# A two-layer decoder trunk: five plain gate/up pairs a layer in place of six, and two plain query/key groups in head one in place of three

## The chip, the cores and the metric

The kernel runs on one core of one Trainium2 chip. The time is the device time of one execution in microseconds (us). A core has TensorE for matmuls (PE in the profile, its weight loads PEld), VectorE (DVE), ScalarE (ACT), GpSimd (POOL) and SyncE (SP), which work side by side, each through its own queue of instructions in order, and 16 DMA engines that move data between HBM and the on-chip memory. Matmuls write to PSUM, of which the kernel keeps eight tiles of 128x512.

## The reference

512 tokens of width 1024 pass through an attention layer and a pooling layer, each followed by a SwiGLU feed-forward net of hidden width 2816. All of it is in float32.

```python
def reference(x, ...):
    for i in range(2):
        if i == 0:
            x = x + dilated_attention_mixer(rmsnorm(x, attn_norm), w_qkv, w_attn_out)
        else:
            x = x + pooling_mixer(rmsnorm(x, pool_norm), w_pool_in, w_pool_group, pool_scale)
        x = x + swiglu_ffn(rmsnorm(x, ffn_norm[i]), w_ffn_gate_up[i], w_ffn_down[i])
    return rmsnorm(x, final_norm)

def swiglu_ffn(h, w_gate_up, w_down):
    gu = h @ w_gate_up
    gate, up = gu[..., :D_FF], gu[..., D_FF:]
    return (jax.nn.silu(gate) * up) @ w_down
```

The attention mixer has eight head slots. Each slot has three groups (dilation 1, 4 and 16) with their own queries, keys and values; the three results of a slot are merged with weights from their softmax denominators, and one output projection follows.

## The kernel before

Activations lie with features on the 128 partitions and the 512 tokens along the columns, in eight tiles of 128 features. To keep nearly float32 accuracy with operands in fp32r, every operand is split into a high and a low half (`split`, L77 on ACT for the high half, L78 on DVE for the low one), and a product is three matmuls: high by high, high by low, low by high.

**Two ways to make a pair of output tiles.** A pair is two tiles of 128 features by 512 tokens: a gate tile and its up tile, or the queries and keys of a group.

- *Plain* (`product`, lines L254 to L257): eight feature tiles times three matmuls of 512 columns for each output tile, 48 matmuls for the pair. Its weights come in two loads of 512 KB (`Plain`, L113) and need two splits of 128x1024.
- *Strassen* (`seven`, `mult`, lines L368 to L370; in the values of attention L481 to L483): the pair, the features and the tokens are each cut in halves, and seven products of half size replace eight. Each is four feature tiles times three matmuls of 256 columns: 84 matmuls. The weights come in three loads by SP (L134 to L136) and one by POOL that adds onto one of them in flight (L137, an accumulating DMA). They need three splits of 128x1024 and one of 128x512, and two additions on DVE between (L150, L151). DVE then joins the seven products (L409, L417, L422, L423).

Strassen also needs sums and differences of the normalized input. `prepare(k)` makes them for feature tiles k and k+4, for k from 0 to 3: two normalizations (L431), three additions (L435 to L437) and their splits (`h` and `t`, `tx` in attention; `tb`, `tt`, `tn` in the feed-forward nets). The scratch of `prepare(k)` is two buffers of the same ring of four that the weights land in (`raw`).

**What sets the order.** `Plain` and `Pair` put their loads and splits in queues when the program is laid out. `pump`, which is called after products, issues the next loads if their buffers are free, and the next split if one of the five buffers for split weights (`w`) is. A scheduler then orders each engine's instructions. In the trace an instruction that waits holds up all behind it on its engine.

**Attention.** Head 0 is plain. In head one the first `NSOLO` groups are plain, the others Strassen; its values and all later heads are Strassen. Between the products other work of the previous and the present head is put in by `between(h, g)`. In head one, after the first group comes `merge(0)`: TensorE exchanges the softmax sums (L618), DVE works out the weights (L620 to L630) and scales head 0's probabilities with them (L632 for `s0`, L635 on ACT for `s12`). At the third group come `turn0(0)`, seven transposes of `s0` on TensorE (L644), `turn12(0)` (L654, L657) and `scores0(1)` (L562 to L573). Behind a plain group these are laid out when both of its products are done. In `seven` they are put behind its first, third and fifth product. `scores12(1)` (L588) stands behind the first product of head one's values.

**Feed-forward net.** Of 22 gate/up pairs a layer the first `NPLAIN` are plain and the others Strassen. Two output tiles and the start of a third are already made before the normalization factor `row` is there (`lead`). `plain_pair` scales gate and up by `row` (L899, L905), and `activation` applies SiLU, multiplies (L868) and splits the result (`a`). `prepare(0)` to `prepare(3)` are laid out behind plain pairs 1 to 4. After 11 pairs the down projection of that half follows.

Of the kernel before, what the change touches and what calls it, by code (L numbers as in the profile page):

```python
# [32 lines left out]
NF = 4  # L33
H2 = S // 2
K2 = KC // 2
NPLAIN = 6
WARM = 6
NSOLO = 3
DOWN = (6, 5)
BUFS = {"w": 5, "half": 2, "raw": 4, "rawhalf": 2}  # L40
COLS = {"w": D, "half": D // 2, "raw": D, "rawhalf": D // 2}
# [7 lines left out]
def trunk(ctx: ExitStack, tc: tile.TileContext, xT, norms, w_first, w_qk, w_qkp, w_v0, w_v0p, w_v12, w_out, w_pair, w_down, w_pin, w_pgrp,  # L49
# [26 lines left out]
    def split(hi, lo, v):  # L76
        nc.scalar.activation(hi, v, AF.Copy)  # L77
        nc.vector.tensor_tensor(lo, v, hi.bitcast(F32), op=OP.subtract)  # L78
# [96 lines left out]
    def pairs(*srcs):  # L175

        these = [Pair(src) for src in srcs]
        for parts in zip(*(p.steps() for p in these)):
            steps.extend(parts)
        units.append(these)  # L180

    def plain_gu(layer, j):
        src = w_pair[layer, j]
        units.extend([Plain(src[:, S:3 * S]), Plain(src[:, 3 * S:], src[:, :S])])

    def plain(*srcs):
        units.extend([Plain(src) for src in srcs])

    for h in range(HEADS):
        if h == 0:  # L190
            plain(*[w_qk[u] for u in range(len(QK) - NF)])
        for g in range(3):
            if h == 1 and g < NSOLO:
                plain(*[w_qk[len(QK) - NF + 2 * g + c] for c in range(2)])
            elif h:
                pairs(w_qkp[3 * h - 3 - NSOLO + g])
        if h == 0:
# [7 lines left out]
    def ffn_plan(layer):  # L205
        for hf in range(2):
            for j in range(hf * HALF, (hf + 1) * HALF):
                if j < NPLAIN:
                    plain_gu(layer, j)
# [55 lines left out]
    def slot(name, dtype=F32R):  # L265
        i = free.popleft()
        t = pools[i].tile([P, 2, S], dtype, tag=f"slot{i}", name=name, bufs=1)
        return i, t
# [3 lines left out]
    def give(key):  # L272
        free.append(held.pop(key))
# [6 lines left out]
    def product(layer):  # L280
        return Product(KC, stream(layer)).add(range(KC)).p
# [23 lines left out]
    def note(layer, k):  # L305

        if layer < 4:
            held[layer, k], t = slot("h")
            scaled(layer, k, t[:, 0], t[:, 1])
        square(layer, k)  # L310
# [115 lines left out]
    def normed(layer, k, row):  # L426

        h, t = Held("raw"), Held("raw")
        for i in range(2):
            c = k + i * K2  # L430
            nc.vector.scalar_tensor_tensor(h.t[:, i * S:(i + 1) * S], X[c], nrm[:, layer, c:c + 1], row,  # L431
                                           op0=OP.mult, op1=OP.mult)
        hq = h.t.rearrange("p (a b c) -> p a b c", a=2, b=2)
        tq = t.t.rearrange("p (a b c) -> p a b c", a=2, b=2)
        nc.vector.tensor_sub(tq[:, :, 0], hq[:, :, 1], hq[:, 0])  # L435
        nc.vector.tensor_sub(t.t[:, H2:S], t.t[:, :H2], h.t[:, 3 * H2:])
        nc.vector.tensor_add(t.t[:, 3 * H2:], t.t[:, H2:S], h.t[:, S:3 * H2])  # L437
        return h, t
# [10 lines left out]
    with tc.tile_pool(name="opool", bufs=1) as opool:  # L449
        early = opool.tile([P, HEADS, S], F32R, tag="o", name="early")  # L450
        with tc.tile_pool(name="apool", bufs=1) as apool:
# [340 lines left out]
            for h in range(1, HEADS):  # L792
                for g in range(3):
                    if h == 1 and g < NSOLO:
                        for c in range(2):
# [58 lines left out]
    with tc.tile_pool(name="fpool", bufs=2) as fpool:  # L854
# [5 lines left out]
        def ftile(name, n=S):  # L860
            return fpool.tile([P, PAD + S], F32, tag="f", name=name, bufs=6)[:, :n]
# [3 lines left out]
        def activation(gt, up):  # L865

            nc.scalar.activation(gt, gt, AF.Silu)
            nc.vector.tensor_mul(up, up, gt)  # L868
            j = len(act)
            held["a", j], t = slot("a")  # L870
            act.append((t[:, 0], t[:, 1]))
            split(*act[-1], up)

        def unfold(m, p):

            if m == 0:
                held["x", 0], t = slot("xs", F32)
                new = t[:, 0]
            else:
                new = x_tile(m - 1)  # L880
            for b in range(NT):
                nc.vector.tensor_add(new[:, b * P:(b + 1) * P], *(
                    t.rearrange("p (r j i b) -> p b i j r", r=NT, j=NT, b=NT)[:, b] for t in (X[m], p)))
            X[m] = new

        def ffn(layer, nxt, lead, row):

            op = nxt - 1

            def gu():  # L890
                return lead.pop(0).p if lead else product(op)

            def hidden(j):
                return act[j]

            def plain_pair(last):
                pg = gu()
                gt = ftile("gt")
                nc.vector.tensor_mul(gt, pg, row)  # L899
                pu = gu()  # L900
                if last:
                    for k in range(KC):
                        give((op, k))
                up = ftile("up")
                nc.vector.tensor_mul(up, pu, row)  # L905
                activation(gt, up)

            T = {}

            def prepare(k):  # L910


                h, t = normed(op, k, row)
                hq, b22 = h.t.rearrange("p (a b c) -> p a b c", a=2, b=2), h.t[:, 3 * H2:]
                held["t", k, 0], b = slot("tb")
                split(b[:, 0].rearrange("p (a c) -> p a c", a=2), b[:, 1].rearrange("p (a c) -> p a c", a=2), hq[:, :, 0])
                T["11", k], T["21", k] = (tuple(b[:, e, i * H2:(i + 1) * H2] for e in range(2)) for i in range(2))
                for i, names in enumerate((("1", "2"), ("3", "4"))):
                    held["t", k, 1 + i], b = slot("tt")
                    split(b[:, 0], b[:, 1], t.t[:, i * S:(i + 1) * S])  # L920
                    for a, name in enumerate(names):
                        T[name, k] = tuple(b[:, e, a * H2:(a + 1) * H2] for e in range(2))
                if k % 2 == 0:
                    held["t", k, 3], T["n"] = slot("tn")
                n = tuple(T["n"][:, e, k % 2 * H2:(k % 2 + 1) * H2] for e in range(2))
                split(*n, b22)
                T["22", k] = n
                h.done()
                t.done()

            def strassen_pair():
                gt, up = ftile("gt"), ftile("up")
                seven(T, gt, up, ftile)
                activation(gt, up)

            for hf in range(2):
                act.clear()
                for j in range(hf * HALF, (hf + 1) * HALF):
                    if j < NPLAIN:
                        plain_pair(j == NPLAIN - 1)  # L940
                        if 0 < j <= K2:
                            prepare(j - 1)
                    else:
                        strassen_pair()
                early = [Product(HALF, hidden).add(range(HALF - 1)) for i in range(2)]
                if hf:
                    for key in [key for key in held if key[0] == "t"]:
                        give(key)
                for m in range(KC - 2 if nxt == 4 and hf else KC):
                    if early:  # L950
                        f = early.pop(0).add([HALF - 1])
                    else:
                        f = Product(HALF, hidden).add(range(HALF))
                    if hf and layer == 0:
                        unfold(m, f.p)
                    else:
                        nc.vector.tensor_add(X[m], X[m], f.p)
                    if hf:
                        note(nxt, m)
                if not (hf and nxt == 4):  # L960
                    for j in range(HALF):
                        give(("a", j))
            return hidden

        lead = begin(2, 1, range(KC - 1))
        row = finish(lead, 1, [KC - 1])
        ffn(0, 2, lead, row)
        moved = x_tile(KC - 1)
        nc.scalar.copy(moved, X[0])
# [73 lines left out]
        for f in lead:  # L1043
            f.add(range(2, 4))
        row = finish(lead, 3, range(2))
        hidden = ffn(1, 4, lead, row)


# [122 lines left out]
```

## Time and profile before

| | |
|---|---|
| median of 3 runs | 1260.09 us (1259.58 to 1260.82) |
| profiled execution | 1261.29 us, span of its instructions 1259.5 us |
| granted TensorE clock, mean | 0.996 |
| PE, PEld, DVE, ACT, POOL busy | 1247.1, 1149.4, 927.3, 563.6, 123.0 us |

Where the stages lie in the span (us from its start), by the matmuls' lines:

| stage | from | to |
|---|---|---|
| head 0 | 0 | 57.45 |
| head one, plain groups 1 to 3 | 57.45 | 90.49 |
| head one, transposes and scores between | 90.49 | 93.13 |
| head one's values, heads 2 to 7 | 93.13 | 438.26 |
| output projection | 438.26 | 489.80 |
| layer 0, plain gate/up pairs | 489.80 | 557.36 |
| layer 0, five Strassen pairs | 557.36 | 607.83 |
| layer 0, down; 11 Strassen pairs; down | 607.83 | 838.44 |
| pooling | 838.44 | 911.98 |
| layer 1, rest of the plain pairs | 911.98 | 964.47 |
| layer 1, five Strassen pairs | 964.47 | 1015.54 |
| layer 1, down; 11 Strassen pairs; down; end | 1015.54 | 1259.5 |

A row of a timeline reads: start, duration, engine, line, operation, output<-inputs, shapes, count, and in brackets how long the engine sat idle before it and what ended that. A matmul's duration is longer than the time it takes in a row of matmuls, since they overlap. So TensorE's pace is read from one start to the next. The same holds on DVE, with smaller overlaps. Rows of a window give busy time and count for each engine, then the granted TensorE clock, the mean busy share of the DMA engines and GB/s.

### The profile page before, as it was taken

How to read it: one execution, taken by the hardware profiler on the slowest of the kernel's cores; microseconds unless marked ns; L12 is line 12 of the kernel's file. 1: busy time of each engine (PE TensorE's matmuls, PEld its weight loads, DVE VectorE, ACT ScalarE, POOL GpSimd, SP SyncE). 2: the span in 40 equal slices, each digit the busy share in tenths (PEclk: the TensorE clock that was granted, in tenths of full speed). 3: DMA queues.
4: the chain of work that ended last, by engine and by line, in shares of the span. 5: the costliest groups of instructions: out<-in, count | busy, mean ns of one | idle time of the engine just before them, and what ended most of it. 6: DMA issues, size and time to landing. Idle time of an engine off the chain costs nothing.

```text
span 1259.5 us, 20807 instructions
## 1 busy us (share of the span) xinstructions
PE 1247.1 (99%) x8262; PEld 1149.4 (91%) x8262; DVE 927.3 (74%) x1415; ACT 563.6 (45%) x871; POOL 123.0 (10%) x121
## 2 busy tenths in 40 slices
PE   9999999999999999999999999999999999999997
PEld 7889999999999988889889999888788988999987
DVE  6987888878879854788537887559878854788643
ACT  6445554544546543445324554343444532455331
POOL 1111111211111100000001110001300000110000
PEclk9999999999999999999999999999999999999998
DMA  8336556656656532246456764333124645676322
GB/s 284 114 85 172 131 158 165 146 144 164 162 143 151 181 122 83 85 112 173 126 142 170 181 180 120 103 134 118 57 72 110 176 125 141 168 187 163 92 69 68
DMA packets 67330, 172.45 MB, mean 137 GB/s; under 512 B 6928, under 2 KB 9120, under 8 KB 67232
## 3 DMA queue, kind: packets, MB, share of 16 engines
q1 hardware_dynamic: 48816, 135.97, 33.6%
q0 software_dynamic: 17264, 34.09, 15.9%
q8 instruction: 65, 1.06, 0.3%
q10 hardware_dynamic: 1152, 1.05, 0.3%
q14 instruction: 33, 0.27, 0.1%
HBM read 168.99 MB, written 2.10 MB: 136 GB/s over the span
## 4 chain that ended last, share of the span: by engine, by line
PE 80%; issue 11%; DVE 6%; DMA 1%; POOL 1%; ACT 1%; SPq 0%; POOLq 0%; DVEq 0%; ACTq 0%
PE ps L369 13%; PE ps L368 13%; PE ps L370 13%; PE ps L254 9%; PE ps L255 9%; PE ps L257 9%; PE ps L481 2%; PE ps L482 2%; PE ps L483 2%; DVE wlo L78 1%; PE ps L678 1%; PE ps L588 1%; DMA raw<-w_pair 1%; DVE n L302 1%; POOL rcol L323 1%
## 5 line engine op out<-in xcount | busy, mean ns | idle before, releaser
L77 ACT ACTIVATE whi<-raw 128x1024 fp32r<-128x1024 f32 (+2 forms) x297 | 296.2, 1002 | 429.3 <-PE ps L255 193.1
L78 DVE TENSOR_TENSOR wlo<-raw,whi 128x1024 fp32r<-128x1024 f32 (+2 forms) x297 | 341.1, 1152 | 137.2 <-ACT whi L77 135.2
L254 PE MATMUL ps<-a,whi 128*128 128x512 f32 (+1 forms) x374 | 141.0, 377 | 0.0
L255 PE MATMUL ps<-a,whi 128*128 128x512 f32 (+1 forms) x374 | 140.9, 377 | 0.0
L257 PE MATMUL ps<-a,wlo 128*128 128x512 f32 (+1 forms) x374 | 140.8, 377 | 0.0
L368 PE MATMUL ps<-tt,whi 128*128 128x256 f32 x384 | 108.7, 283 | 0.0
L369 PE MATMUL ps<-tt,whi 128*128 128x256 f32 x384 | 108.7, 283 | 0.0
L370 PE MATMUL ps<-tt,wlo 128*128 128x256 f32 x384 | 108.7, 283 | 0.0
L137 POOL DMA_DIRECT2D raw<-w_pair x32 | 38.7, 1210 | 445.9 <-DVE wlo L78 182.3
L257 PEld LDWEIGHTS ps<-a,wlo 128*128 128x128 f32 x374 | 70.4, 188 | 13.0
L254 PEld LDWEIGHTS ps<-a,whi 128*128 128x128 f32 x374 | 70.4, 188 | 12.7
L255 PEld LDWEIGHTS ps<-a,whi 128*128 128x128 f32 x374 | 70.4, 188 | 12.7
L368 PEld LDWEIGHTS ps<-tt,whi 128*128 128x128 f32 x384 | 73.7, 192 | 0.0
L369 PEld LDWEIGHTS ps<-tt,whi 128*128 128x128 f32 x384 | 73.7, 192 | 0.0
L370 PEld LDWEIGHTS ps<-tt,wlo 128*128 128x128 f32 x384 | 73.7, 192 | 0.0
L369 PE MATMUL ps<-tb,whi 128*128 128x256 f32 x256 | 72.6, 284 | 0.4 <-DVE tb L78 0.4
L368 PE MATMUL ps<-h,whi 128*128 128x256 f32 x252 | 72.5, 288 | 0.0
L370 PE MATMUL ps<-tb,wlo 128*128 128x256 f32 x256 | 72.4, 283 | 0.0
L368 PE MATMUL ps<-tb,whi 128*128 128x256 f32 x256 | 72.4, 283 | 0.0
L370 PE MATMUL ps<-h,wlo 128*128 128x256 f32 x252 | 71.3, 283 | 0.0
L369 PE MATMUL ps<-h,whi 128*128 128x256 f32 x252 | 71.3, 283 | 0.0
L254 PE MATMUL ps<-h,whi 128*128 128x512 f32 x160 | 62.7, 392 | 0.0
(281 smaller groups left out, 3412.8 us busy)
## 6 DMA issues: line engine op xcount, KB each, us to landing
raw<-w_pair SPq DMA_DIRECT2D x76, 512.0 KB, 4.4
raw<-w_qkp SPq DMA_DIRECT2D x36, 512.0 KB, 4.1
raw<-w_pair POOLq DMA_DIRECT2D x32, 512.0 KB, 7.3
raw<-w_down SPq DMA_DIRECT2D x32, 384.0 KB, 3.1
raw<-w_down SPq DMA_DIRECT2D x32, 320.0 KB, 2.8
raw<-w_v SPq DMA_DIRECT2D x18, 512.0 KB, 4.4
raw<-w_qkp POOLq DMA_DIRECT2D x18, 512.0 KB, 7.2
rawhalf<-w_pair SPq DMA_DIRECT2D x32, 256.0 KB, 3.3
```

Source lines behind the costliest of these rows:

```text
L77: nc.scalar.activation(hi, v, AF.Copy)
L78: nc.vector.tensor_tensor(lo, v, hi.bitcast(F32), op=OP.subtract)
L137: nc.gpsimd.dma_start(self.b.t.rearrange("p (a c) -> p a c", a=2), self.src[:, None, 3 * S:].to_broadcast([P, 2, S]), accum_op=OP.add)
L254: nc.tensor.matmul(self.p[:, cols], w[0][:, s], mh[:, cols], start=self.done == 0, stop=False)
L255: nc.tensor.matmul(self.p[:, cols], w[0][:, s], ml[:, cols], start=False, stop=False)
L257: nc.tensor.matmul(self.p[:, cols], w[1][:, s], mh[:, cols], start=False, stop=self.done == self.n)
L368: nc.tensor.matmul(dst, w.t[0][:, c], th, start=k == 0, stop=False)
L369: nc.tensor.matmul(dst, w.t[0][:, c], tl, start=False, stop=False)
L370: nc.tensor.matmul(dst, w.t[1][:, c], th, start=False, stop=k == K2 - 1)
L481: nc.tensor.matmul(o, mh, wh, start=k == 0, stop=False)
L482: nc.tensor.matmul(o, mh, wl, start=False, stop=False)
L483: nc.tensor.matmul(o, ml, wh, start=False, stop=k == K2 - 1)
```

## The change

`NPLAIN` goes from 6 to 5: gate/up pair 5 of each layer is made by Strassen. `prepare(0)` to `prepare(3)` are laid out behind plain pairs 0 to 3. `NSOLO` goes from 3 to 2: the third group of head one (dilation 16) is made by Strassen.

```diff
-NPLAIN = 6
+NPLAIN = 5
 WARM = 6
-NSOLO = 3
+NSOLO = 2
...
                     if j < NPLAIN:
                         plain_pair(j == NPLAIN - 1)
-                        if 0 < j <= K2:
-                            prepare(j - 1)
+                        if j < K2:
+                            prepare(j)
                     else:
                         strassen_pair()
```

The three places at which instructions move, engine by engine:

TensorE, end of head one's third group, before (`s_509` is head 0's `s0`, `L254` to `L257` the plain product):

```order
L254 MATMUL ps<-early,whi 128x512
L255 MATMUL ps<-early,whi 128x512
L257 MATMUL ps<-early,wlo 128x512
L644 MATMUL ps<-ident,s_509 128x128 x7
L654 MATMUL ps<-ident,s_598 128x128 x4
L562 MATMUL ps<-qk_699,qk_668 128x256 x2
```

The same seven transposes now (`s_512` is `s0`):

```order
L368 MATMUL ps<-h,whi 128x256
L369 MATMUL ps<-h,whi 128x256
L370 MATMUL ps<-h,wlo 128x256
L644 MATMUL ps<-ident,s_512 128x128 x7
L368 MATMUL ps<-h,whi 128x256
```

They stood behind all 48 matmuls of the group. Now they stand behind its first 12, ahead of the other 72.

DVE, from the scores of head 0 to the scaling of `s0`, before. The first rows are those around the third `prepare` of attention (L431, `h`), then come those just ahead of the scaling:

```order
L590 SCALAR_TENSOR_TENSOR s_598<-ps,b_504 128x512
L431 SCALAR_TENSOR_TENSOR raw<-x,nrm,row 128x512 x2
L590 SCALAR_TENSOR_TENSOR s_598<-ps,b_504 128x512
L78 TENSOR_TENSOR h<-raw,h 128x512 x2
L595 TENSOR_REDUCE st<-s_598 128x4
L596 TENSOR_SCALAR nm<-st 128x4
L459 TENSOR_TENSOR qk_668<-ps,row 128x4x32x4
```

And now:

```order
L590 SCALAR_TENSOR_TENSOR s_601<-ps,b_507 128x512 x2
L150 TENSOR_TENSOR raw<-raw 128x512
L595 TENSOR_REDUCE st<-s_601 128x4
L151 TENSOR_TENSOR raw<-raw 128x512
L596 TENSOR_SCALAR nm<-st 128x4
L459 TENSOR_TENSOR qk_664<-ps,row 128x4x32x4
L606 TENSOR_TENSOR far<-st,place 128x64
L78 TENSOR_TENSOR wlo<-raw,whi 128x1024
L431 SCALAR_TENSOR_TENSOR raw<-x,nrm,row 128x512 x2
L78 TENSOR_TENSOR h<-raw,h 128x512 x2
```

The third `prepare` moved behind the evacuation of the first group's queries (L459) and behind a split of Strassen weights, whose buffer it takes. From that L459 up to the first L632 there are now two L431, two `h` and one `wlo` more than before, and one L151 less.

DVE in layer 0 of the feed-forward nets, around the third `prepare` (L431), before:

```order
L905 TENSOR_TENSOR up<-ps,row 128x512
L868 TENSOR_TENSOR up<-up,gt 128x512
L78 TENSOR_TENSOR wlo<-raw,whi 128x1024
L78 TENSOR_TENSOR a<-up,a 128x512
L150 TENSOR_TENSOR raw<-raw 128x512
L151 TENSOR_TENSOR raw<-raw 128x512
L899 TENSOR_TENSOR gt<-ps,row 128x512
L78 TENSOR_TENSOR wlo<-raw,whi 128x1024
L431 SCALAR_TENSOR_TENSOR raw<-x,nrm,row 128x512 x2
```

And now:

```order
L868 TENSOR_TENSOR up<-up,gt 128x512
L78 TENSOR_TENSOR wlo<-raw,whi 128x1024
L78 TENSOR_TENSOR a<-up,a 128x512
L899 TENSOR_TENSOR gt<-ps,row 128x512
L150 TENSOR_TENSOR raw<-raw 128x512
L431 SCALAR_TENSOR_TENSOR raw<-x,nrm,row 128x512 x2
L151 TENSOR_TENSOR raw<-raw 128x512
L905 TENSOR_TENSOR up<-ps,row 128x512
```

The third `prepare` stands one pair earlier. The first Strassen pair's weights are loaded ahead of the first `prepare` in place of behind the second, so L150 works on older data. From the second pair's L905 to the last `tb` (of `prepare(3)`) there were 55 rows and are now 50: two `wlo`, one L905, one L868 and one `a` fewer. Layer 1 has the same order.

## Prediction, on record before the changed kernel ran

> **What bounds the kernel now.** I read the page first, then the chain of waits, then the windows of the stages.
>
> ```profile
> span 1259.5 us, 20807 instructions
> PE 1247.1 (99%) x8262; PEld 1149.4 (91%) x8262; DVE 927.3 (74%) x1415; ACT 563.6 (45%) x871; POOL 123.0 (10%) x121
> ...
> PE 80%; issue 11%; DVE 6%; DMA 1%; POOL 1%; ACT 1%; SPq 0%; POOLq 0%; DVEq 0%; ACTq 0%
> ```
>
> TensorE is busy for 99% of the span and holds 80% of the chain, so each matmul saved counts, unless TensorE then waits. A busy PE is not yet PE at its pace, so I take the pace from windows that hold nothing but one kind of product (PE busy, count, clock, DMA share, GB/s).
>
> ```profile
> 79.53:90.49 10.96, 10.96 (x50) 1.00 0.54 139
> 504.87:557.36 52.49, 52.49 (x234) 1.00 0.33 88
> 557.36:607.83 50.47, 50.47 (x421) 1.00 0.63 172
> ```
>
> The first is head one's third group, 48 matmuls of 512 columns: 10.96 us. The second holds 231 of the feed-forward kind (the count takes in some at the edges): 52.49/231 = 0.227, a plain pair 48 x 0.227 = 10.91. The third is five Strassen pairs: 50.47/5 = 10.09, and 50.47/420 = 0.120 for a matmul. So a pair gains only 0.82, because 84 short matmuls take nearly as long as 48 long ones. All three changed groups together are worth about 2.4 us, 0.19%. What decides is whether TensorE waits.
>
> **The group in head one.** TensorE now, where the third group ends:
>
> ```profile
> 90.49 0.93 PE L644 MATMUL ps<-ident,s 128*128 128x128 f32 x7
> 91.25 0.60 PE L654 MATMUL ps<-ident,s 128*128 128x128 f32 x4
> ...
> 93.13 0.36 PE L481 MATMUL ps<-whi,h 128*128 128x256 f32 x1
> 93.33 0.28 PE L482 MATMUL ps<-wlo,h 128*128 128x256 f32 x1
> ...
> 96.08 1.95 PE L588 MATMUL ps<-qk,qk 128*128 128x128 f32 x16
> ```
>
> The transposes, turn12 and the scores take 93.13 - 90.49 = 2.64, as before. A Strassen product that comes after other matmuls starts with one step of 0.20 in place of 0.12 (93.13 to 93.33). That now happens three times in place of once, 0.16 in all. The group gains 10.96 - 10.09 - 0.16 = 0.71.
>
> The price is that the transposes (L644, 91.25 - 90.49 = 0.76) now stand behind the first 12 short matmuls, at 79.53 + 12 x 0.12 = 80.97. They need `s0` scaled by L632. DVE's rows before:
>
> ```profile
> 58.61 1.41 DVE L431 SCALAR_TENSOR_TENSOR raw<-x,nrm,row 128x512 f32<-128x512 f32 x2
> 59.93 0.69 DVE L590 SCALAR_TENSOR_TENSOR s<-ps,b 128x512 f32<-128x512 f32 x1
> ...
> 63.21 1.12 DVE L459 TENSOR_TENSOR qk<-ps,row 128x512 f32<-128x512 f32 x1
> 65.33 0.23 DVE L606 TENSOR_TENSOR far<-st,place 128x64 f32<-128x64 f32 x1 [0.99 <-ACT s L599]
> 66.28 1.23 DVE L78 TENSOR_TENSOR wlo<-raw,whi 128x1024 fp32r<-128x1024 f32 x1 [0.72 <-ACT whi L77]
> ...
> 72.52 1.22 DVE L78 TENSOR_TENSOR wlo<-raw,whi 128x1024 fp32r<-128x1024 f32 x1
> 73.66 0.68 DVE L435 TENSOR_TENSOR raw<-raw 128x512 f32<-128x512 f32 x1
> 74.26 0.68 DVE L78 TENSOR_TENSOR h<-raw,h 128x512 fp32r<-128x512 f32 x1
> ...
> 79.11 0.68 DVE L151 TENSOR_TENSOR raw<-raw 128x512 f32<-128x512 f32 x1
> ...
> 81.03 1.40 DVE L632 TENSOR_SCALAR s<-s,co 128x256 f32<-128x256 f32 x4
> ```
>
> L459 at 63.21 waits for TensorE in both orders, so it stays where it is. From there to the first L632 the new order has two L431 more (59.93 - 58.61 = 1.32), two `h` (2 x 0.60, the step from 73.66 to 74.26), one `wlo` (73.66 - 72.52 = 1.14), and one L151 less (0.60): 3.06 more. Of the old idle time, 0.99 + 0.72, I take 1.1 as gone, since the exponentials that L606 waits for now start about a microsecond earlier, and the split still waits for ACT. L632 starts at 81.03 + 3.06 - 1.1 = 83.0 and its four end at 84.4; the last transposes end TensorE's step at about 84.5. Without a wait it would be 80.97 + 0.76 = 81.73. TensorE loses **2.8**. Bounds: with no idle time gone it is 3.9; with all of it gone and another microsecond saved by rows that no longer wait for the one just before them it is 1.2.
>
> The accumulating load that L150 now waits for ahead of L459 could hold up this chain:
>
> ```profile
> 46.24 0.33 SPq L113 DMA_DIRECT2D raw<-w_qk  x1
> ...
> raw<-w_v POOLq DMA_DIRECT2D x2, 512.0 KB, 6.6
> raw<-w_qkp SPq DMA_DIRECT2D x6, 512.0 KB, 4.9
> ...
> 938.70 8.23 DMA raw<-w_pair
> ```
>
> Its first load goes out in the slot of the one at 46.24 and lands 4.9 later, at 51.1. The accumulation takes 6.6 to 8.2 more and lands at 57.7 to 59.3. DVE reaches L150 at about 59.2, and L459 has another 1.3 us to spare behind it. I cost it at nothing; each microsecond past 60.6 would add one.
>
> A second wait: the scores at L588 need L422 of the new group, and DVE's rows ahead of it hang on the next accumulating load.
>
> ```profile
> 92.83 0.69 DVE L563 SCALAR_TENSOR_TENSOR s<-ps,b 128x512 f32<-128x512 f32 x1
> ...
> 95.26 0.26 DVE L573 TENSOR_SCALAR nm<-st 128x4 f32<-128x4 f32 x1
> ```
>
> That load starts when `prepare(3)` frees its buffer, by the same count about 79.6, and its two parts take 4.9 + 6.6: 91.1. Up to L422 DVE then has the scores (95.26 - 92.83 = 2.43), two `wlo` (2.28) and five rows of 0.60 with 0.2 between them: 7.9, which ends at 99.0. TensorE arrives at 93.13 + 2.8 - 0.71 + (96.08 - 93.13) = 98.2. I take half of the 0.8, **0.4**, for loads that land a little sooner; the bounds are 0 and 1.5. Head one: -0.71 + 2.8 + 0.4 = **+2.5**.
>
> **The feed-forward pairs.** What counts is when the last `tb` is there, since the tenth and later matmuls of the first Strassen pair read it. Before (windows with DVE alone, then rows):
>
> ```profile
> 514.04:557.81 43.77, 37.07 (x56) 1.00 0.31 73
> 921.15:965.50 44.35, 37.08 (x55) 1.00 0.29 72
> ...
> 535.80 0.69 DVE L905 TENSOR_TENSOR up<-ps,row 128x512 f32<-128x512 f32 x1 [1.23 <-PE ps L257]
> 542.59 0.69 DVE L150 TENSOR_TENSOR raw<-raw 128x512 f32<-128x512 f32 x1 [3.47 <-issue]
> 547.89 0.69 DVE L78 TENSOR_TENSOR tb<-raw,tb 128x512 fp32r<-128x512 f32 x1 [0.70 <-ACT tb L77]
> 557.81 0.68 DVE L78 TENSOR_TENSOR tb<-raw,tb 128x512 fp32r<-128x512 f32 x1
> ...
> 558.43 0.28 PE L368 MATMUL ps<-tb,whi 128*128 128x256 f32 x1
> 558.55 0.38 PE L369 MATMUL ps<-tb,whi 128*128 128x256 f32 x1
> 558.77 0.27 PE L370 MATMUL ps<-tb,wlo 128*128 128x256 f32 x1
> ...
> 965.54 0.28 PE L368 MATMUL ps<-tb,whi 128*128 128x256 f32 x1
> 966.24 0.39 PE L369 MATMUL ps<-tb,whi 128*128 128x256 f32 x1 [0.42 <-DVE tb L78]
> ```
>
> In layer 0 the `tb` came just in time (0.10 lost after 558.55); in layer 1 TensorE lost 966.24 - 965.54 - 0.12 = 0.58. So the old kernel has no slack here, and now TensorE asks 10.91 earlier. From the second pair's L905 at 514.04 to the last `tb` DVE worked 37.07 and idled 6.70. Five rows go: two `wlo` at 1.14 and three of 0.60, 4.08 in all, leaving 32.99. The idle time at L150 and at L905 goes too, for the load is older and TensorE is ahead. What is left is some 1.0, the wait for ACT and small ones. The last `tb` starts at 514.04 + 32.99 + 1.0 = 548.0 and ends at 548.7. TensorE wants it at 557.36 - 10.91 + 10 x 0.12 = 547.65, so it waits 1.1. Rows that stand apart from what they depend on save perhaps 0.7 of this. I take **0.7** a layer, between 0 and 3.4 (half of the old idle time stays). The `tt` that the third product wants come about as late as TensorE then is. Layer 0: -0.82 + 0.7 - 0.1 = -0.2. Layer 1: -0.82 + 0.7 - 0.58 = -0.7.
>
> The three more POOL issues, the extra loads and ACT's extra splits lie beside TensorE: POOL is busy 10%, ACT 45%. DVE's four joining rows in place of two evacuations lie behind the product they belong to.
>
> **The sum.** +2.5 - 0.2 - 0.7 = +1.6. Against the profiled execution's own 1261.29 (1259.5 of span and 1.8 around it) that is 1262.9. That execution lies 1.2 above the median of the runs shown, so on the median 1260.09 it is **1261.7**.
>
> **The rivals.**
> - *Slower, the blocks come late.* If DVE in the feed-forward nets keeps half of its idle time, TensorE waits 3.4 in place of 0.7 at the first Strassen pair of each layer: 1261.7 + 5.4 = 1267.1. Past a wait of 1.2 a layer the change is slower by over 0.2%. For it: 37.07 of 43.77 were busy, and layer 1 already waited. Against it: the longest idle time, 3.47, is one whose cause moves away.
> - *The clock falls in the gap.* TensorE would stand still from 81.0 to about 83.4. Windows at the end of the span, all engines:
>
> ```profile
> 1246.00:1250.00 4.00, 3.34 (x29) 3.26 (x28) 2.93 (x8) 0.42 (x1) 0.00 (x0) 1.00 0.75 245
> 1250.00:1259.50 9.50, 2.18 (x9) 1.80 (x9) 2.60 (x7) 0.39 (x1) 2.11 (x3) 0.53 0.36 120
> ```
>
> The clock held at 1.00 with short gaps and fell to 0.53 where TensorE stood still most of the time. Half the clock for as long as the gap loses 1.2, and such a gap is longer than mine by 1 or more: about 1264. Page "TensorE: Matmul & The Clock Gate" of the Trainium skill, section "Why this matters for your kernels", puts the edge at gaps over about 3 us; by that the clock would hold at 2.4, and the sum stays. No row here shows the edge.
> - *Faster.* If the scaling of `s0` is done by 81 and the blocks come in time, nothing is lost: -0.71 - 0.82 - 0.1 - 0.82 - 0.58 = -3.0, 1257.1. With waits half as long, 1259.4. Against it: the five rows more ahead of L632 stand in the order above. That order also rules out that the change leaves the work as it was.
>
> **How the numbers follow.** The forecast has 0.62, by itself 1259.8 to 1263.7; late blocks 0.18; the clock 0.08; faster 0.12. The range of 8 in 10 is 1259.0 to 1265.0. With 0.2%, 2.5 us, as what a measurement of this kernel can tell from no change, the forecast is within it for 0.51 of its 0.62 and slower for 0.11. Late blocks (0.16) and the clock (0.08) are mostly slower. Of the faster case half passes the bound. That makes 0.06 faster, 0.59 within, 0.35 slower.
>
> **What would show it.** In the changed kernel's rows TensorE idles 2 to 3 us ahead of head one's seven L644, released by DVE L632, with an L632 at about 83. At the first L369 on the last `tb` of each layer it waits 0.4 to 1.1. Strassen pairs keep 10.09. If the L644 run on without a wait, or the wait at `tb` is over 1.2, the forecast is wrong. Should L150 ahead of L459 wait past 60.6, its cause is the load.

## The result and the profile after

The changed kernel takes 1263.89 us (median of 8 runs, 1262.75 to 1264.79), the kernel before 1260.28 (8 runs). The ratio is 1.0029, with a 95% interval of 1.0019 to 1.0038: slower by 0.29%, 3.6 us. The forecast was 1261.7. The time lies within the forecast's range, but 2.2 us above the point, where one of the rivals stood ("the clock falls in the gap", about 1264, chance 0.08). The 3.6 us are also more than the 2.5 that the forecast took as no change, for which it had a chance of 0.59; slower than that had 0.35.

The page of the changed kernel, its first lines and its chain of waits:

```profile
span 1261.8 us, 21087 instructions
PE 1246.5 (99%) x8370; PEld 1154.2 (91%) x8370; DVE 936.3 (74%) x1433; ACT 567.6 (45%) x880; POOL 127.8 (10%) x124
...
PE 73%; issue 12%; DVE 10%; DMA 2%; POOL 1%; ACT 1%; SPq 0%; DVEq 0%; POOLq 0%; ACTq 0%
```

TensorE works 0.6 us less in a span that is 2.3 longer, and DVE has 10% of the chain in place of 6%. So the time went into waits of TensorE, above all for DVE. The windows of the stages show where. Before:

```profile
0.00:57.45 57.45, 55.02 (x253) 45.02 (x253) 45.46 (x70) 31.15 (x48) 7.32 (x11) 1.00 0.61 209
57.45:93.13 35.68, 35.68 (x169) 29.77 (x167) 31.09 (x54) 18.67 (x39) 5.24 (x5) 1.00 0.36 84
93.13:607.83 514.70, 514.57 (x3870) 494.31 (x3869) 407.48 (x627) 253.38 (x429) 61.15 (x65) 1.00 0.55 144
607.83:1015.54 407.71, 405.86 (x2435) 362.82 (x2433) 299.36 (x464) 173.66 (x239) 33.20 (x25) 1.00 0.46 129
1015.54:1259.50 243.96, 235.99 (x1548) 217.48 (x1546) 143.95 (x204) 86.73 (x118) 16.10 (x15) 0.98 0.46 125
```

The same five stages in the changed kernel:

```profile
0.00:56.96 56.96, 55.46 (x252) 46.01 (x253) 45.34 (x70) 30.99 (x48) 8.98 (x12) 1.00 0.61 203
56.96:97.83 40.87, 36.81 (x205) 32.45 (x204) 33.13 (x59) 20.18 (x41) 6.26 (x7) 0.96 0.38 101
97.83:611.89 514.06, 513.88 (x3905) 495.32 (x3904) 411.35 (x634) 254.87 (x433) 61.13 (x65) 1.00 0.55 146
611.89:1018.83 406.94, 405.30 (x2471) 363.78 (x2470) 302.48 (x470) 175.04 (x242) 35.36 (x26) 1.00 0.47 132
1018.83:1261.80 242.97, 235.06 (x1548) 216.65 (x1546) 144.00 (x204) 86.54 (x118) 16.09 (x15) 0.99 0.46 125
```

Head one's three groups, with the transposes and scores (second row), cost 5.19 more, and in no other row did TensorE's mean clock fall below what it was. The stage with layer 0's gate/up pairs gains 0.64, the one with layer 1's gains 0.77. That is +3.8, close to the 3.6 of the medians. In the first and the last stage TensorE's work is the same in both kernels, and their 0.49 and 0.99 are not put down to the change: head 0 took 56.2 to 57.45 us in all the profiles but one (the loads held back, below), and in the last stage the clock fell 9.0 us ahead of the end before (at 1250.52) and 5.7 ahead of it now (at 1256.12).

TensorE at the third group of head one, in the changed kernel (timeline):

```profile
80.42 0.28 PE L370 MATMUL ps<-h,wlo 128*128 128x256 f32 x1
84.76 1.49 PE L644 MATMUL ps<-ident,s 128*128 128x128 f32 x7 [4.06 <-DVE s L632]
85.90 0.56 PE L368 MATMUL ps<-h,whi 128*128 128x256 f32 x1
...
86.90 0.41 PE L369 MATMUL ps<-h,whi 128*128 128x256 f32 x1
87.11 0.41 PE L370 MATMUL ps<-h,wlo 128*128 128x256 f32 x1
...
90.12 0.60 PE L654 MATMUL ps<-ident,s 128*128 128x128 f32 x4
```

And its windows there:

```profile
84.76:85.90 1.14, 1.14 (x7) 0.95 (x8) 1.14 (x4) 1.14 (x4) 0.40 (x1) 0.76 0.92 320
85.90:87.00 1.10, 1.10 (x7) 1.10 (x6) 0.75 (x2) 0.69 (x2) 0.84 (x1) 0.50 0.21 86
87.00:88.50 1.50, 1.50 (x9) 1.50 (x9) 0.00 (x0) 0.85 (x1) 0.00 (x0) 0.50 0.61 98
```

The wait for the scaled `s0` is there, as the prediction placed it, but it is longer: from 80.42 + 0.12 = 80.54 to 84.76, 4.2 us. The profile's 4.06 counts from the modelled end of the last matmul. Then comes a second loss: the granted clock is 0.50, matmuls step by 0.21 in place of 0.12 (86.90 to 87.11), the transposes take 85.90 - 84.76 = 1.14 in place of 0.76, and the 24 products behind them 4.22 in place of 24 x 0.12 + 0.08 = 2.96. The clock takes 0.38 + 1.26 = 1.6. Head one is then -0.71 + 4.2 + 1.6 = +5.1, and 5.19 was measured.

DVE's rows say why `s0` was late:

```profile
61.26 0.69 DVE L150 TENSOR_TENSOR raw<-raw 128x512 f32<-128x512 f32 x1 [2.45 <-issue]
61.87 1.21 DVE L595 TENSOR_REDUCE st<-s 128x4 f32<-128x1024 f32 x1
...
65.91 0.23 DVE L606 TENSOR_TENSOR far<-st,place 128x64 f32<-128x64 f32 x1 [1.14 <-ACT s L599]
...
84.36 1.07 DVE L632 TENSOR_SCALAR s<-s,co 128x256 f32<-128x256 f32 x4
```

The first L150 idles 2.45 until the accumulating load is there (issued by POOL at 50.36, landed 10.8 later, at 61.2). L595 and the exponentials behind it start later by as much, so L606 still waits 1.14 for them: the idle time that I had taken as gone stays. The loads issued from 44 to 66, with the time to their landing, and the row of the issue:

```profile
50.36 1.40 POOL L137 DMA_DIRECT2D raw<-w_qkp  x1 [18.73 <-DVE raw L437]
...
raw<-w_v SPq DMA_DIRECT2D x2, 512.0 KB, 9.0
raw<-w_qkp POOLq DMA_DIRECT2D x1, 512.0 KB, 10.8
```

The accumulating load (`w_qkp` by POOL) took 10.8 us, where I had reckoned with 6.6 to 8.2. Beside it ran the first two loads of the value weights (`w_v`), which SP issued 1.6 and 2.2 us after it.

In the feed-forward nets, TensorE at the last `tb` of layer 0 in the changed kernel:

```profile
552.18 0.28 PE L368 MATMUL ps<-tb,whi 128*128 128x256 f32 x1
552.51 0.39 PE L369 MATMUL ps<-tb,whi 128*128 128x256 f32 x1
```

The step is 0.33 in place of 0.12: it loses 0.2 there, and as much in layer 1.

### The profile page after: what moved, and what is told of

Same layout as the page of the kernel before. It is cut to its first block, busy times and chain, and to the rows that moved or that the text cites. A ratio compares the mean times of both kernels' runs of the same rounds, so it can differ in the third digit from the quotient of the medians.

```text
span 1261.8 us, 21087 instructions
## 1 busy us (share of the span) xinstructions
PE 1246.5 (99%) x8370; PEld 1154.2 (91%) x8370; DVE 936.3 (74%) x1433; ACT 567.6 (45%) x880; POOL 127.8 (10%) x124
## 4 chain that ended last, share of the span: by engine, by line
PE 73%; issue 12%; DVE 10%; DMA 2%; POOL 1%; ACT 1%; SPq 0%; DVEq 0%; POOLq 0%; ACTq 0%
PE ps L369 14%; PE ps L368 14%; PE ps L370 14%; PE ps L254 7%; PE ps L255 7%; PE ps L257 7%; DVE wlo L78 2%; PE ps L481 2%; PE ps L482 2%; PE ps L483 2%; DVE raw L431 1%; PE ps L678 1%; PE ps L588 1%; POOL rcol L323 1%; DVE raw L435 1%
## 5 line engine op out<-in xcount | busy, mean ns | idle before, releaser
L78 DVE TENSOR_TENSOR wlo<-raw,whi 128x1024 fp32r<-128x1024 f32 (+2 forms) x300 | 344.6, 1152 | 147.1 <-ACT whi L77 146.1
L254 PE MATMUL ps<-a,whi 128*128 128x512 f32 (+1 forms) x374 | 141.0, 377 | 0.0
L257 PE MATMUL ps<-a,wlo 128*128 128x512 f32 (+1 forms) x374 | 140.8, 377 | 0.0
L368 PE MATMUL ps<-tt,whi 128*128 128x256 f32 x408 | 115.5, 283 | 0.0
L369 PE MATMUL ps<-tt,whi 128*128 128x256 f32 x408 | 115.5, 283 | 0.0
L370 PE MATMUL ps<-tt,wlo 128*128 128x256 f32 x408 | 115.5, 283 | 0.0
L257 PEld LDWEIGHTS ps<-a,wlo 128*128 128x128 f32 x374 | 70.4, 188 | 12.9
L254 PEld LDWEIGHTS ps<-a,whi 128*128 128x128 f32 x374 | 70.4, 188 | 12.8
L368 PEld LDWEIGHTS ps<-tt,whi 128*128 128x128 f32 x408 | 78.3, 192 | 0.0
L369 PEld LDWEIGHTS ps<-tt,whi 128*128 128x128 f32 x408 | 78.3, 192 | 0.0
L370 PEld LDWEIGHTS ps<-tt,wlo 128*128 128x128 f32 x408 | 78.3, 192 | 0.0
L369 PE MATMUL ps<-tb,whi 128*128 128x256 f32 x272 | 77.2, 284 | 0.1
L370 PE MATMUL ps<-tb,wlo 128*128 128x256 f32 x272 | 77.0, 283 | 0.0
L368 PE MATMUL ps<-tb,whi 128*128 128x256 f32 x272 | 76.9, 283 | 0.0
L368 PE MATMUL ps<-h,whi 128*128 128x256 f32 x264 | 76.6, 290 | 0.0
L370 PE MATMUL ps<-h,wlo 128*128 128x256 f32 x264 | 75.2, 285 | 0.0
L369 PE MATMUL ps<-h,whi 128*128 128x256 f32 x264 | 75.2, 285 | 0.0
L254 PE MATMUL ps<-h,whi 128*128 128x512 f32 x144 | 56.4, 392 | 0.0
```

What stands on the lines that cost most here:

```text
L254: nc.tensor.matmul(self.p[:, cols], w[0][:, s], mh[:, cols], start=self.done == 0, stop=False)
L257: nc.tensor.matmul(self.p[:, cols], w[1][:, s], mh[:, cols], start=False, stop=self.done == self.n)
L368: nc.tensor.matmul(dst, w.t[0][:, c], th, start=k == 0, stop=False)
L369: nc.tensor.matmul(dst, w.t[0][:, c], tl, start=False, stop=False)
L370: nc.tensor.matmul(dst, w.t[1][:, c], th, start=False, stop=k == K2 - 1)
```

## The experiments

Ten runs follow, of eight kernels, with 4 to 11 executions each. The kernel before ran beside them on the same chip (its medians: 1260.0 to 1260.2).

**One part alone, head one.** The kernel before with `NSOLO` alone changed.

```diff
-NSOLO = 3
+NSOLO = 2
```

> Only the third group of head one is Strassen; six plain pairs a layer and the old place of prepare stay. By my reading of the two traces the whole loss is here: TensorE waits about 4.1 us at the seven transposes of s0, loses about 1.7 more at half clock, and gains 0.7 of product time, +5.1 in all, so 1265.4 against 1260.3 before. If head one costs only what I had forecast (+2.5), it is 1262.8, and the rest of the loss must come from the feed-forward pairs.

Measured: 1266.63, ratio 1.0049 (1.0035 to 1.0063). Its stage of head one takes 5.4 more than before, with a wait of 4.33 at L644 and half clock behind it. Between the two profiles that is the whole loss (1266.63 against 1261.29). The medians differ by 6.5, as the profiled execution of the kernel before lies 1.0 above its median. The median lies 1.2 above my number; in its profile the load landed later still, 11.3 us after its issue.

**The other part alone, the feed-forward nets.** The changed kernel with `NSOLO = 3`, run twice.

```diff
-NPLAIN = 6
+NPLAIN = 5
...
-                        if 0 < j <= K2:
-                            prepare(j - 1)
+                        if j < K2:
+                            prepare(j)
```

> Only the feed-forward part: five plain pairs a layer and prepare one pair sooner; head one has its three plain groups. By the rows of the two traces layer 0 gains 0.6 and layer 1 gains 1.2, so -1.75: 1258.5 against 1260.3. By my forecast (a wait of 0.7 a layer) it gains 0.9: 1259.4. If the blocks are late and cost what the pair gains, it is 1260.3 or more.

> Only the feed-forward part of the change, once more, to see whether its gain is larger than the measurement's uncertainty. From the stages of its first profile: layer 0 -0.56, layer 1 -0.72, so 1258.9 against 1260.2. If the first result (0.08% faster) was chance, 1260.2.

Measured: 1259.21, ratio 0.9992 (0.9983 to 1.0001), and 1259.01, ratio 0.9991 (0.9981 to 1.0000). Windows of the first, up to the end of each layer's Strassen pairs:

```profile
92.32:606.46 514.14, 513.96 (x3906) 495.40 (x3905) 410.07 (x632) 254.16 (x432) 62.45 (x66) 1.00 0.56 145
606.46:1013.44 406.98, 405.32 (x2471) 363.78 (x2470) 303.00 (x471) 174.72 (x242) 35.36 (x26) 1.00 0.49 133
```

Against 514.70 and 407.71 that is -0.56 and -0.73, a gain of 1.3 by the rows and about 1.0 by the medians. Both intervals just reach no change; that the gain is real rests on two runs and the rows together. This is the fastest of all the kernels here, though by less than 0.2%.

**Is it the clock?** 24 matmuls more, right ahead of the seven transposes.

```diff
                     p = ps()
+                    for i in range(24 if h == 0 and lo == 0 else 0):
+                        nc.tensor.matmul(p[:, :H2], T["11", 0][0][:, :P], T["11", 0][0], start=True, stop=True)
                     for a in range(n):
```

> The changed kernel with 24 more matmuls of 256 columns on TensorE right ahead of the seven transposes; their result is overwritten. They take 24 x 0.12 = 2.9 us of the 4.1 us in which TensorE waits, and leave an idle gap of 1.2. If the slow rows behind the gap are the clock, which falls because TensorE stood still for 4 us, the clock stays at 1.00, the transposes take 0.76 in place of 1.14, the 24 products behind them lose nothing in place of 1.35, and the kernel takes 1263.9 - 1.7 = 1262.2. If the rows are slow for another reason (operands or weights that come late), nothing changes: 1263.9.

Measured: 1265.72 (1261.79 to 1266.02), ratio 1.0034 (1.0021 to 1.0047). The profiled execution was the one at 1261.79, and there the load landed early (9.1 us after its issue). DVE, then TensorE (two lines were added, so the transposes are L646):

```profile
58.56 0.69 DVE L150 TENSOR_TENSOR raw<-raw 128x512 f32<-128x512 f32 x1 [0.55 <-DVE s L590]
...
81.66 1.07 DVE L632 TENSOR_SCALAR s<-s,co 128x256 f32<-128x256 f32 x4
```

```profile
79.73 3.04 PE L644 MATMUL ps<-h 128*128 128x256 f32 x24
82.62 0.93 PE L646 MATMUL ps<-ident,s 128*128 128x128 f32 x7
```

It says nothing of the slow rows behind the transposes, as no long gap was left there, but much of the load. From L150 to L632 it is 81.66 - 58.56 = 23.10 us here and 84.36 - 61.26 = 23.10 in the changed kernel; in three more profiles with this order it is 23.09, 23.09 and 23.10. So there is no slack between them: each microsecond by which the load lands later, TensorE waits longer. With the load in time, L632 stands 81.66 - 56.17 = 25.5 behind the start of head one's first group, where the prediction had 83.0 - 57.45 = 25.5. The count of DVE's rows was right, and the load's landing was not. The next two runs are the changed kernel and the one with the extra matmuls again, side by side.

> The changed kernel once more, as the control on the chip of this group: 1263.9, with TensorE idle about 4 us ahead of the seven L644 and half clock behind them. The landing of the accumulating load (L150 ahead of L459) may differ between executions; each microsecond earlier than 61.2 should shorten the wait by one.

> The changed kernel with 24 more matmuls ahead of the seven transposes, again. In the earlier profile the accumulating load landed early (by 58.6), so there was no long gap for the extra matmuls to fill, and the profile says nothing of the clock. If the load lands late (61 or later) in this one, the extra matmuls leave a gap of about 1 us: with the clock as the cause of the slow rows the clock holds at 1.00 and the transposes take 0.76; with another cause they take 1.14 and the next 24 products lose 1.3 again. Time by the clock: 1.0 to 1.7 under the control of this group, less what the wait at L588 takes back (0 to 1.7); by another cause: equal to the control.

Measured: 1264.79, ratio 1.0037 (1.0024 to 1.0049), for the changed kernel, with the load landing after 11.6 us and TensorE idle for 4.52 ahead of L644; 1264.72, ratio 1.0040 (1.0026 to 1.0053), with the extra matmuls. In the latter's profile the load was late (L150 at 60.71), and TensorE's rows are:

```profile
84.22 1.14 PE L646 MATMUL ps<-ident,s 128*128 128x128 f32 x7 [1.07 <-DVE s L632]
...
87.82 0.28 PE L369 MATMUL ps<-tx,whi 128*128 128x256 f32 x1
87.94 0.28 PE L370 MATMUL ps<-tx,wlo 128*128 128x256 f32 x1
...
100.82 2.85 PE L588 MATMUL ps<-qk,qk 128*128 128x128 f32 x14 [1.80 <-DVE qk L422]
```

With the gap cut to 1.07 the products behind it keep their pace (87.82 to 87.94) and the clock stays at 1.00, so the slow rows hang on the idling, and not on operands that come late. The median alone would not tell the two apart, as it equals the control's. Nothing is won, for TensorE now comes earlier to L588, waits 1.80 there for L422, and the clock falls at that place (windows):

```profile
101.00:102.00 1.00, 1.00 (x8) 1.00 (x9) 0.70 (x2) 0.51 (x2) 0.37 (x1) 0.70 1.05 145
102.00:103.00 1.00, 1.00 (x6) 1.00 (x6) 0.69 (x1) 0.00 (x0) 0.00 (x0) 0.50 0.93 139
```

**Prepare without the pair's buffers, and the load alone.** The first loads of head one's value weights (`units[9]`) are held back until the third and fourth `prepare` are laid out.

```diff
-            while loads and all(room(r, c) for r, c in loads[0][1].items()):
+            while loads and loads[0][0] not in gate and all(room(r, c) for r, c in loads[0][1].items()):
...
+    gate.extend(units[9])
     plain(*[w_out[m] for m in range(KC)])
...
+            gate.clear()
             scores12(0)
```

> The changed kernel, but the loads of head one's value weights are held back until the third and fourth prepare are laid out. So these two prepares no longer take the scratch buffers that the weights of the Strassen pairs hold, and the accumulating load of the third group runs without the value loads beside it. If the late third and fourth prepare and the late load make s0 late, the accumulating load lands near 57 to 58 in place of 61.2 (6.6 to 7.5 after its issue in place of 10.8), s0 is scaled before TensorE asks, the 4.1 us at L644 go, and the clock holds. The first evacuations of head one then stand behind both prepares, which can cost about 1 us at the exchange of the softmax sums. Forecast: 1263.9 - 5.8 + 1 = 1259.1, between 1258.0 and 1260.0. If the wait comes from the work on DVE as such and not from whom it stands behind, the wait moves but stays: 1262 or more.

Measured: 1265.26, ratio 1.0039 (1.0026 to 1.0051). The load landed 7.8 us after its issue, without the value loads beside it, as expected.

```profile
raw<-w_qkp POOLq DMA_DIRECT2D x1, 512.0 KB, 7.8
```

The wait at L644 is gone too. But a wait came up at the end of head 0 (two lines were added, so L540 is L538 of the changed kernel):

```profile
61.59 1.11 PE L540 MATMUL ps<-ident,vt 128*128 128x128 f32 x4 [5.88 <-DVE vt L461]
```

The third `prepare` now ran ahead of the second evacuation of head 0's values (L461), which TensorE needs at once, and the clock was at 0.50 from 59.42 to 66.25. So the rival's forecast held: the wait moved and stayed, at 1262 or more. That DVE simply has too much work there is not shown: from 50 to 85 it was busy for 31.18 us here, for 30.58 in the changed kernel, and for 31.95 in the kernel before, where TensorE hardly waited. What differs is which rows stand ahead of the one that TensorE needs. This edit moves the `prepare` and the neighbours of the load at once, so it does not price the load alone.

**The transposes later.**

```diff
+                if h == 1 and g == 2:
+                    return {4: [later(turn0, 0)], 5: [later(turn12, 0)], 6: [later(scores0, 1)]}
```

> The changed kernel, but in head one's third group the seven transposes are laid out behind the fifth Strassen product (TensorE there at 79.1 + 60 x 0.12 = 86.3, later than the scaled s0 at 85.4), the four of turn12 behind the sixth and the scores behind the seventh. The wait at L644 goes and the values begin near 92.0 in place of 97.8. Then the second wait of my forecast should show: the scores of the other groups (L588) come at about 94.9 and need L422, which stands behind a split of value weights whose accumulating load lands near 92.2: L422 ends at about 98, a wait of about 3 at L588, and perhaps a fall of the clock behind it. Forecast 1261.4 to 1262.7. If L588 does not wait, 1258.0; if the lateness is of TensorE's other operands, the wait stays in the third group and the time at 1263.9.

Measured: 1261.85, ratio 1.0012 (1.0003 to 1.0021), 2.9 under the changed kernel on the same chip. The wait at L644 is gone, and two others stand in its place:

```profile
93.58 0.39 PE L481 MATMUL ps<-whi,h 128*128 128x256 f32 x1 [1.85 <-ACT t L645]
97.91 1.83 PE L588 MATMUL ps<-qk,qk 128*128 128x128 f32 x14 [0.95 <-DVE qk L422]
```

I had expected one of about 3 at L588. The larger one came by another way: the copies of the transposes (L645) stand on ACT behind a split that waits for the values' accumulating load, and until they are done TensorE's next product does not start (L481 writes a PSUM tile, and its releaser is L645).

```profile
92.00 1.06 ACT L77 ACTIVATE whi<-raw 128x1024 fp32r<-128x1024 f32 x1 [2.86 <-DMA raw<-w_v]
92.97 0.95 ACT L645 COPY t<-ps 128x512 f32<-128x512 f32 x2
```

**The old place of prepare**, with five plain pairs and `NSOLO = 3`.

```diff
-                        if j < K2:
-                            prepare(j)
+                        if 0 < j <= K2:
+                            prepare(j - 1)
```

> Five plain pairs a layer, three plain groups in head one, and prepare in its old place, behind pairs 1 to 4. The last tb then stands on DVE behind the last plain pair's L905, which needs TensorE's last plain matmul (551.1), and four rows more: about 555.3, where TensorE wants it at 552.3. A wait of 3.0 a layer in place of 0.2, so +5.6 against the same kernel with the prepare one pair sooner (1259.2): 1264.8, and up to 1266.8 if the clock falls in these gaps. If the place of prepare does not matter, 1259.2.

Measured: 1259.47, ratio 0.9992 (0.9984 to 1.0001), the same as with the earlier place. DVE and TensorE in layer 0, where the first Strassen pair begins at 545.57:

```profile
549.44 0.69 DVE L78 TENSOR_TENSOR tb<-raw,tb 128x512 fp32r<-128x512 f32 x1
```

```profile
549.89 0.28 PE L369 MATMUL ps<-tt,whi 128*128 128x256 f32 x1
550.18 0.39 PE L369 MATMUL ps<-tb,whi 128*128 128x256 f32 x1
```

The last `tb` is indeed late: it starts at 549.44, and in the laid-out order TensorE would read it at about 546.8. But the scheduler had reordered TensorE too: the matmuls on that `tb`'s low half stand behind matmuls of later products, on `tt`, and lose about 0.2. My 3.0 came from DVE's order alone, with TensorE's taken as unchanged.

**One pair fewer still**: `NPLAIN = 4`, `NSOLO = 3`, new place of prepare.

```diff
-NPLAIN = 5
+NPLAIN = 4
```

> Four plain pairs a layer, prepare behind pairs 0 to 3, head one with three plain groups. One more pair a layer gains 0.82. The last prepare now stands behind the last plain pair on DVE: from that pair's L905 to the last tt are some 17 rows, about 11 us, and TensorE has other matmuls of the first Strassen pair for about 7. If the scheduler's interleaving hides what it can, a wait of 3 to 4 a layer stays: 1258.9 + 2 x (3.5 - 0.8) = 1264.3. If it hides all, 1257.3, the fastest so far.

Measured: 1273.48, ratio 1.0110 (1.0094 to 1.0126). The scheduler reorders again, and this time it isn't enough:

```profile
547.88 0.74 PE L368 MATMUL ps<-tb,whi 128*128 128x256 f32 x4 [2.88 <-ACT tb L77]
551.84 0.39 PE L370 MATMUL ps<-tt,wlo 128*128 128x256 f32 x1 [0.70 <-DVE wlo L78]
```

The seven Strassen pairs of layer 0 take 78.1 in place of 7 x 10.13 = 70.9, about 7 lost a layer, more than my 3 to 4. One of the waits, 0.70, is for DVE's split of the next weights; the rest was not taken apart. Of four, five and six plain pairs, five is the best.

## Why the prediction was right or wrong

- **What the groups gain (0.71 and 0.82 a pair): right.** Strassen pairs kept their pace: six of them in 551.11 to 611.89, 10.13 each with the wait for the last `tb` in it, and 10.09 was forecast.
- **Head one, the wait at L644: the place and the releaser right, 4.2 in place of 2.8.** The step that failed is "I cost it at nothing" for the accumulating load ahead of L459, in both its halves. The landing was estimated at 57.7 to 59.3 from the medians of such loads; it took 10.4 to 11.6 us in five of six profiles with the value loads beside it, 9.1 in one, and 7.8 with those held back. And the "1.3 us to spare" at L459 do not exist: the chain to `s0` runs from L150 through L595 and the exponentials, and follows L150 at 23.1 us. The prediction did name this load as the cause should L150 wait past 60.6, and L150 stood at 61.26. With that, L632 came 1.9 later than forecast, counted from the start of head one's first group; 0.4 goes against it, since the transposes begin behind the first of the four L632 (84.36 + 0.40) and not with the last. The rest of that step, the rows counted from L459 to L632, was right to 0.1, as the execution with the early load shows.
- **The clock: I gave it 0.08, and it fell.** The rival's condition was a gap longer than mine by 1 or more, and that is what the late load made of it. It cost 1.6 in the changed kernel, and 1.2 was forecast. The Trainium skill's page "TensorE: Matmul & The Clock Gate", section "Why this matters for your kernels", puts the edge at gaps over about 3 us; the falls behind 4.06 and 4.33 agree with it, those behind 1.80 and, once of twice, 2.88 do not. The chance was too small even for the forecast's own gap of 2.4: by the steps of 3.41 us in the last section, a gap of 2.4 leaves 1.8 or more in one step at about two of three positions (an estimate from the rows there).
- **The second wait, at L588: 0 in place of 0.4.** TensorE came too late to wait. It is real all the same: 1.80 as soon as the first wait is shortened, so taking away the wait at L644 alone does not give back all that head one lost.
- **The feed-forward nets: -0.2 and -0.7 forecast, about -0.6 and -0.75 measured.** The wait for the last `tb` was about 0.2 a layer in place of 0.7, the lower part of its bounds: DVE reached that `tb` 33.1 us behind the second pair's L905 (518.66 to 551.77), where 34.0 was worked out. That layer 1 came out at its number is luck. With a wait of 0.2 its terms give -0.82 + 0.2 - 0.58 = -1.2; 0.4 of this went at the end of the pooling, where POOL's L323, which TensorE's L331 needs, took 1.97 us in place of 1.02. This L323 took 1.96 to 1.98 in all the other profiles, with the old feed-forward part as well, so the 1.02 belongs to one execution of the kernel before. The 0.58 does not stand in every execution either: in the profile with head one alone changed, the old feed-forward part waits 0.5 for the last `tb` in layer 0 and not at all in layer 1.
- **The sum.** That the time fell inside the range says little for the working: +2.5 - 0.2 - 0.7 = +1.6 was forecast, +5.2 - 0.6 - 0.8 = +3.8 measured by the stages. Of the 2.2 us between them, the late load has 1.9 and the clock 1.6, less 0.4 at the transposes' start, 0.4 at L588 and 0.5 in the feed-forward nets.

## What to carry to other kernels

A load that is put at nothing because it lands "in time" needs its own row in the new order: look which transfers will run beside it, and which chain, not which neighbouring row, hangs on it. When a wait of TensorE grows to two microseconds or more, reckon with half clock behind it, and before a wait is removed, see what the next engine has ready: of the two cures here, holding the loads back gave all of the time back at another place, and the later transposes won 2.9 us but still left the kernel 1.7 slower than before. Where a scheduler orders all engines, read the order of the waiting engine as well as that of the late one.

## What the runs showed of the hardware

- After TensorE idled 4.06 us the clock was granted at 0.50 from 85.36 to 88.77, for 3.41 us, and then at 1.00 again. It fell ahead of the kernel's end in six profiles, for 3.4 us in four of them and for 6.8 in two. In each of the six, the fall at the kernel's end lies a whole number of steps of 3.413 us behind the first (85.36 and 1256.12 are 343 steps apart). So the clock changes at the edges of steps that run by themselves, and a gap's length alone does not decide: what counts is how much of it lies in one step. Counted back from a fall of the same execution (idle is the window's length less TensorE's busy time in it):

| kernel | step | idle in it | clock in the next step |
|---|---|---|---|
| changed kernel, gap of 4.06 | 81.93 to 85.35 | 2.83 | 0.50 |
| four plain pairs, layer 0, gap of 2.88 | 543.10 to 546.51 | 1.52 | 1.00 |
| the same gap | 546.51 to 549.92 | 1.37 | 1.00 |
| four plain pairs, layer 1, gap of 2.88 | 959.52 to 962.94 | 2.10 | 0.50 |
| transposes later, gap of 1.85 | 89.61 to 93.03 | 1.30 | 1.00 |
| 24 matmuls more, first run, gap of 1.73 | 96.42 to 99.83 | 1.73 | 1.00 |
| 24 matmuls more, second run, gap of 1.80 | 98.00 to 101.41 | 1.80 | 0.50 |

In all the profiles here, between 20 and 1235 us, every step with 1.80 us idle or more was followed by half clock and none with 1.73 or less was. Idle time is not the whole measure: at the kernel's end, among sparse work, 1.07 was enough. The Trainium skill ("TensorE: Matmul & The Clock Gate", section "What's actually happening") has the activity judged in windows of about 3.4 us that run by themselves; the steps agree with that.

- The same accumulating load of 512 KB took 7.8 us with no value loads beside it (one profile, in which DVE's rows were moved too) and 9.1 to 11.6 with two of 512 KB beside it (six profiles). POOL issued the one and SP the others: issuing from another engine seems not to have kept them apart. The Trainium skill says so too ("DMA: Bandwidth & Descriptors", section "Issuing engines are not separate DMA queues").
- The landing differs by up to 2.5 us between executions with the same loads; why is open. In the kernel with 24 more matmuls, five executions lie between 1261.8 and 1266.0; only the fastest has a trace, and there the load came early. That the load is late in the others is inferred, not seen.
